# Series of unread matrix products added behind the last store of an encoder kernel

## The chip, the cores and the metric

The kernel runs on one core of a Trainium2 chip. The metric is the device time of one execution in microseconds (us). Before the change it was 1070.83 us, the median of two runs (1070.76 and 1070.89).

## The reference, cut to what matters

The reference is a bidirectional encoder of two layers over 256 tokens of width 1024, in f32:

```
for l in range(2):
    x = x + 0.5 * swiglu(rms_norm(x, ffn1_norm[l]), ffn1_w_in[l], ffn1_w_out[l])
    h = rms_norm(x, mix_norm[l])
    x = x + mixers(h) @ w_mix_out[l]         # latent, windowed and neighbourhood attention
    x = x + mem_xattn(rms_norm(x, mem_norm_x[l]), mem, ...)
    x = x + 0.5 * swiglu(rms_norm(x, ffn2_norm[l]), ffn2_w_in[l], ffn2_w_out[l])
    x = rms_norm(x, block_norm[l])
return x
```

Only its last line bears on the change: after the second feed-forward of layer 1, `x` is divided by the root of its mean square and returned.

## The kernel before, in words

The activations live in SBUF, transposed, as `x` of 128 partitions x 8 blocks x 256 tokens, a view of the tile `gx`. The weights stream in as pieces of 128x1024; ScalarE casts each to a high part in fp32r (L140, `whi`) and VectorE makes the low part (L141, `wlo`). A product of f32 accuracy is three TensorE products in fp32r (`mm3`, L167 to L169). In the feed-forward layers (`ffn`, names f01, f02, f11, f12) each of them loads 128x128 weights that lie side by side and streams 256 columns; in one projection of the mixer (`formb`, mb1) 512 columns. A weight load is an instruction of its own (LDWEIGHTS, shown as the engine PEld) that runs beside the product ahead of it.

Sums over partitions are f32 products with a column of constants (L979). `pacc` has eight PSUM banks of 512 f32 columns, which `acc(name)` hands out; `sp` has ten SBUF slots of 8 KB per partition, which `slot` hands out. During the last feed-forward eight of the ten slots are held by its input (two) and its inner activations (six).

The end of the kernel, L974 to L992, is one chain: the sum of squares (L979), its mean (L984), the power of -1/2 on GpSimd (L173), the transposition of the factor (L988), and five products of `x` with it on VectorE (L991), each followed by a store of its blocks by SyncE's queue (L992). `x` is complete in SBUF only after the fifth.

At the very start four products of zeros fill a bank that nothing reads (L117 to L119, name `idle`).

A framework orders the instructions of each engine from the dependences between tiles and a simulated timeline (L1126), and sets the semaphores. Where the profile gives L1126, it means the framework's waits and the barrier at the end.

Of the kernel before, what the change touches and what calls it, by code (L numbers as in the profile page):

```python
# [10 lines left out]
F32R = mybir.dt.float32r  # L11
# [7 lines left out]
P = 128  # L19
T = 256  # L20
# [971 lines left out]
        nc.sync.dma_start(out[:, a:b, :], v)  # L992

def _tiles(v):

    return v.reshape(-1, P).T
# [132 lines left out]
```

## Time and profile before

| | |
|---|---|
| median of the runs | 1070.83 us |
| the profiled execution's own time | 1071.27 us |
| its span, first to last instruction | 1069.5 us |
| mean granted TensorE clock | 0.994 of full |
| TensorE products, busy | 1048.8 us, 8480 instructions |
| weight loads, busy | 1027.0 us, 8480 instructions |
| VectorE busy | 717.6 us |
| ScalarE busy | 556.9 us |

The span is 1.77 us shorter than the profiled execution's own time. Busy times of products and of weight loads overlap, and a product's busy time is longer than the distance between two starts, since they are pipelined: the distance between starts is what a series costs.

### The profile page before, as it was taken

The numbers are of one execution on the slowest core, as the hardware profiler recorded it, in microseconds if no ns is written. First come the engines' busy times: TensorE is split into PE (matmuls) and PEld (weight loads), VectorE is DVE, ScalarE is ACT, GpSimd is POOL, SyncE is SP. The second block draws the span as 40 slices with busy tenths as digits, with TensorE's granted clock in tenths as the row PEclk, the third lists the DMA queues.
The fourth block names the chain that finished last, engine by engine and source line by source line (L and its number), as shares of the span: only waits on it lengthen the run. The fifth ranks groups of instructions, "written<-read, shape, count | busy, mean of one in ns | idle before, by whom it ended". The sixth has DMA issues, their size and how long they took to land.

```text
span 1069.5 us, 20916 instructions
## 1 busy us (share of the span) xinstructions
PE 1048.8 (98%) x8480; PEld 1027.0 (96%) x8480; DVE 717.6 (67%) x1249; ACT 556.9 (52%) x928; POOL 114.5 (11%) x107
## 2 busy tenths in 40 slices
PE   8999999999999999999999999999999999999996
PEld 7999999988999999999999999999889999999996
DVE  7866666678786676666658666667886776666652
ACT  5644455566554554445445444546674545544441
POOL 4000000071020500000000000001500321000000
PEclk9999999999999999999999999999999999999998
DMA  8865556555041655555555555655631426656641
GB/s 290 269 191 183 193 189 205 172 180 179 21 138 60 229 185 182 193 179 194 181 180 188 184 190 187 205 181 165 192 111 46 153 78 215 187 191 183 190 122 40
DMA packets 54530, 181.79 MB, mean 170 GB/s; under 512 B 6049, under 2 KB 8993, under 8 KB 54433
## 3 DMA queue, kind: packets, MB, share of 16 engines
q1 hardware_dynamic: 54432, 180.45, 52.7%
q8 instruction: 66, 1.08, 0.4%
q14 instruction: 32, 0.25, 0.1%
HBM read 179.38 MB, written 1.05 MB: 169 GB/s over the span
## 4 chain that ended last, share of the span: by engine, by line
PE 75%; issue 17%; DVE 4%; DMA 2%; ACT 1%; POOL 1%; SPq 0%; POOLq 0%; DVEq 0%; ACTq 0%
PE f11i L167 4%; PE f01i L167 4%; PE f01i L169 4%; PE f11i L169 4%; PE f11i L168 3%; PE f01i L168 3%; PE f02i L167 3%; PE f02i L169 3%; PE f02i L168 3%; PE f11o L167 2%; PE f02o L167 2%; PE f01o L167 2%; PE f11o L169 2%; PE f02o L169 2%; PE f01o L169 2%
## 5 line engine op out<-in xcount | busy, mean ns | idle before, releaser
L141 DVE TENSOR_TENSOR wlo<-raw,whi 128x1024 fp32r<-128x1024 f32 (+4 forms) x337 | 406.8, 1211 | 227.6 <-ACT whi L140 226.6
L140 ACT CAST whi<-raw 128x1024 fp32r<-128x1024 f32 (+4 forms) x337 | 343.7, 1023 | 372.9 <-issue 92.6
L167 PE MATMUL f02i<-n20h,whi 128*128 128x256 f32 x320 | 90.5, 283 | 0.0
L168 PE MATMUL f12i<-n21l,whi 128*128 128x256 f32 x320 | 90.2, 282 | 0.0
L167 PE MATMUL f12i<-n21h,whi 128*128 128x256 f32 x320 | 90.2, 282 | 0.0
L168 PE MATMUL f02i<-n20l,whi 128*128 128x256 f32 x320 | 90.1, 281 | 0.0
L169 PE MATMUL f02i<-n20h,wlo 128*128 128x256 f32 x320 | 90.0, 281 | 0.0
L169 PE MATMUL f12i<-n21h,wlo 128*128 128x256 f32 x320 | 90.0, 281 | 0.0
L167 PE MATMUL f11i<-n10h,whi 128*128 128x256 f32 x320 | 89.9, 281 | 0.0
L167 PE MATMUL f01i<-n0h,whi 128*128 128x256 f32 x320 | 89.8, 281 | 0.0
L169 PE MATMUL f01i<-n0h,wlo 128*128 128x256 f32 x320 | 89.4, 279 | 0.0
L168 PE MATMUL f01i<-n0l,whi 128*128 128x256 f32 x320 | 89.3, 279 | 0.0
L169 PE MATMUL f11i<-n10h,wlo 128*128 128x256 f32 x320 | 89.3, 279 | 0.0
L168 PE MATMUL f11i<-n10l,whi 128*128 128x256 f32 x320 | 89.3, 279 | 0.0
L169 PEld LDWEIGHTS f02i<-n20h,wlo 128*128 128x128 f32 x320 | 61.0, 191 | 0.0
L167 PEld LDWEIGHTS f12i<-n21h,whi 128*128 128x128 f32 x320 | 60.9, 190 | 0.0
L168 PEld LDWEIGHTS f12i<-n21l,whi 128*128 128x128 f32 x320 | 60.9, 190 | 0.0
L167 PEld LDWEIGHTS f02i<-n20h,whi 128*128 128x128 f32 x320 | 60.8, 190 | 0.0
L168 PEld LDWEIGHTS f02i<-n20l,whi 128*128 128x128 f32 x320 | 60.6, 189 | 0.0
L169 PEld LDWEIGHTS f12i<-n21h,wlo 128*128 128x128 f32 x320 | 60.6, 189 | 0.0
L169 PEld LDWEIGHTS f01i<-n0h,wlo 128*128 128x128 f32 x320 | 60.2, 188 | 0.0
L169 PEld LDWEIGHTS f11i<-n10h,wlo 128*128 128x128 f32 x320 | 60.2, 188 | 0.0
(1026 smaller groups left out, 2945.1 us busy)
## 6 DMA issues: line engine op xcount, KB each, us to landing
raw<-in_w SPq DMA_DIRECT2D x311, 512.0 KB, 3.9
raw<-in_w SPq DMA_DIRECT2D x12, 384.0 KB, 3.3
raw<-in_w SPq DMA_DIRECT2D x8, 416.0 KB, 3.3
kv0mt<-in_mem SPq DMA_DIRECT2D x8, 128.0 KB, 4.2
kv1mt<-in_mem SPq DMA_DIRECT2D x8, 128.0 KB, 3.9
gx<-in_gx SPq DMA_DIRECT2D x3, 256.0 KB, 6.2
out<-gx SPq DMA_DIRECT2D x3, 256.0 KB, 2.8
gx<-in_gx SPq DMA_DIRECT2D x1, 323.0 KB, 3.1
```

Source lines behind the costliest of these rows:

```text
L140: ins = nc.scalar.copy(hi[:, a:b], r[:, a:b])
L141: nc.vector.tensor_tensor(lo[:, a:b], r[:, a:b], hi[:, a:b].bitcast(F32), ALU.subtract)
L167: nc.tensor.matmul(ps, ah, bh, start=first, stop=False)
L168: nc.tensor.matmul(ps, ah, bl, start=False, stop=False)
L169: return nc.tensor.matmul(ps, al, bh, start=False, stop=last)
```

## The change

Nothing of the old code is changed. Behind the last store two slots, `sr` and `mr`, are filled with copies of the finished `x` in fp32r by VectorE. Then TensorE runs series of products: the weights are 128 columns of `sr` taken with a step `s` in elements of 4 bytes, the moving operand is `n` columns of `mr` that begin `m` bytes into it. Each series accumulates into one bank, and nothing reads the banks.

| series | number | step s | columns n | products each | products |
|---|---|---|---|---|---|
| heat | 1 | 1 | 512 | 24 | 24 |
| za | 4 | 1 | 256 | 24 | 96 |
| zb | 16 | 2 | 256 | 12 | 192 |
| zc | 8 | 2 | 512 | 10 | 80 |
| zd | 8 | 4 | 256 | 10 | 80 |
| ze | 4 | 3 | 256 | 10 | 40 |
| zf | 4 | 1 | 512 | 12 | 48 |
| zg | 8 | 2 | 256 | 12 | 96 |

```diff
         nc.sync.dma_start(out[:, a:b, :], v)
 
 
+    sr = slot([P, 8, T], F32R, "sr")
+    mr = slot([P, 8, T], F32R, "mr")
+    for d_ in (sr, mr):
+        nc.vector.tensor_copy(d_, x)
+    st, mv = sr.rearrange("p k t -> p (k t)"), mr.rearrange("p k t -> p (k t)")
+
+    def series(name, w, s, m, n, reps, step, mod):
+        ps = acc(name)
+        for i in range(reps):
+            o = w + (i * step) % mod
+            lhs = st[:, o : o + 128 * s].rearrange("p (c s) -> p c s", s=s)[:, :, 0]
+            nc.tensor.matmul(
+                ps[:, 0:n], lhs, mv[:, m // 4 : m // 4 + n], start=i == 0, stop=i == reps - 1
+            )
+
+    series("heat", 0, 1, 0, 512, 24, 128, 1024)
+    for m in (0, 64, 128, 192):
+        series(f"zaw0s1m{m}n", 0, 1, m, 256, 24, 128, 1024)
+    for w in (0, 1):
+        for m in range(0, 256, 32):
+            series(f"zbw{w}s2m{m}n", w, 2, m, 256, 12, 256, 1536)
+    for m in range(0, 256, 32):
+        series(f"zcw0s2m{m}n", 0, 2, m, 512, 10, 256, 1536)
+    for m in (0, 32, 64, 96, 128, 160, 192, 224):
+        series(f"zdw0s4m{m}n", 0, 4, m, 256, 10, 1, 4)
+    for m in (0, 64, 128, 192):
+        series(f"zew0s3m{m}n", 0, 3, m, 256, 10, 1, 3)
+    for m in (0, 64, 128, 192):
+        series(f"zfw0s1m{m}n", 0, 1, m, 512, 12, 128, 1024)
+
+    for m in range(0, 256, 32):
+        ps = acc(f"zgm{m}")
+        for i in range(12):
+            o = (i // 2) * 256 + i % 2
+            lhs = st[:, o : o + 255].rearrange("p c -> p c")[:, 0:255:2] if o % 2 else st[:, o : o + 256 : 2]
+            nc.tensor.matmul(ps[:, 0:256], lhs, mv[:, m // 4 : m // 4 + 256], start=i == 0, stop=i == 11)
```

## Rows read from the trace of the kernel before

**Rows 1.** The page: busy time, share, instructions of PE; clock in 40 slices.
```profile
PE 1048.8 (98%) x8480; PEld 1027.0 (96%) x8480; DVE 717.6 (67%) x1249; ACT 556.9 (52%) x928; POOL 114.5 (11%) x107
...
PEclk9999999999999999999999999999999999999998
```

**Rows 2.** Timeline of the end: start us, us, engine, line, operation, count.
```profile
1062.04 0.43 PE L988 MATMUL endb<-ident,endr 128*128 128x128 f32 x2 [1.03 <-POOL endr L173]
1062.51 2.54 DVE L991 TENSOR_TENSOR gx<-gx,endb 128x256 f32<-128x256 f32 x5 [1.30 <-PE endb L988]
1062.95 2.45 SPq L992 DMA_DIRECT2D out<-gx  x5
```

**Rows 3.** The stores' line: issue ns min/median/max, first and last start; time to landing.
```profile
L992 SPq DMA_DIRECT2D out<-gx x5: 332/338/423, 1063.0 to 1065.1; - x5
...
DMA to landing us min/median/max: 1.9/2.5/3.0
```

**Rows 4.** Stretches at the end: busy by engine (count), clock, DMA share, GB/s.
```profile
1062.00:1063.00 1.00, 0.43 (x2) 0.19 (x2) 0.49 (x2) 0.00 (x0) 0.00 (x0) 0.97 0.00 0
1063.00:1064.00 1.00, 0.00 (x0) 0.00 (x0) 1.00 (x3) 0.00 (x0) 0.00 (x0) 0.50 0.17 58
...
1066.00:1069.50 3.50, 0.00 (x0) 0.00 (x0) 0.00 (x0) 0.00 (x0) 0.00 (x0) 0.50 0.34 101
```

**Rows 5.** VectorE's groups by form: busy us, mean ns of one, idle before.
```profile
L991 DVE TENSOR_TENSOR gx<-gx,endb 128x512 f32<-128x512 f32 x3 | 1.9, 681 | 0.0
...
L852 DVE TENSOR_SCALAR mx0o<-mx0o,mx0or 128x256 f32<-128x256 f32 x4 | 1.2, 350 | 0.4 <-POOL mx0or L173 0.3
...
L852 DVE TENSOR_SCALAR mx0o<-mx0o,mx0or 128x512 f32<-128x512 f32 x2 | 0.9, 484 | 0.8 <-POOL mx0or L173 0.8
L991 DVE TENSOR_TENSOR gx<-gx,endb 128x256 f32<-128x256 f32 x2 | 0.8, 419 | 1.3 <-PE endb L988 1.3
```

**Rows 6.** The tile f12o, its 528 products: ns min/median/max, first and last start.
```profile
L167 PE MATMUL f12o<-f12ah,whi x176: 279/279/280, 996.6 to 1058.5; 128*128 128x256 f32 x176
...
L169 PE MATMUL f12o<-f12ah,wlo x176: 279/279/281, 996.9 to 1058.7; 128*128 128x256 f32 x176
```

**Rows 7.** Timeline of mb1, first and last of 13 products of 512 columns.
```profile
227.68 0.40 PE L530 MATMUL mx0mb<-whi,nx0l 128*128 128x512 f32 x1
...
230.48 0.40 PE L530 MATMUL mx0mb<-whi,nx0l 128*128 128x512 f32 x1
```

**Rows 8.** Timeline of PEld: four weight loads under products of one column.
```profile
1058.70 0.53 PEld L979 LDWEIGHTS end<-cmean,nb1s 128*128 128x128 f32 x4
```

**Rows 9.** The tile endb: its weights are one element read 128 times.
```profile
L988 PEld LDWEIGHTS endb<-ident,endr x2: 132/134/136, 1062.0 to 1062.1; 128*128 128x128 f32 x2
```

**Rows 10.** PEld's groups by form: transpositions with weights side by side.
```profile
L739 PEld LDWEIGHTS mx0st<-ident,mx0qk 128*128 128x128 f32 x14 | 1.6, 140 | 0.1
```

**Rows 11.** Timeline of PE at two falls of the clock (15 starts after 888.87).
```profile
362.21 0.61 PE L251 MATMUL n20ps<-cmean,n20s 128*128 128x1 f32 x4 [1.68 <-POOL n20s L208]
...
886.96 0.61 PE L251 MATMUL n21ps<-cmean,n21s 128*128 128x1 f32 x4 [2.15 <-POOL n21s L208]
...
888.87 0.42 PE L167 MATMUL f12i<-n21h,whi 128*128 128x256 f32 x1
...
892.08 0.37 PE L167 MATMUL f12i<-n21h,whi 128*128 128x256 f32 x1
```

**Rows 12.** Stretches there: the clock stands behind POOL's count.
```profile
366.50:367.00 0.50, 0.50 (x6) 0.50 (x6) 0.00 (x0) 0.00 (x0) 0.00 (x0) 0.88 0.57 205
...
889.00:892.00 3.00, 3.00 (x16) 3.00 (x15) 0.72 (x1) 0.54 (x1) 0.00 (x0) 0.50 0.84 289
892.00:892.50 0.50, 0.50 (x5) 0.50 (x4) 0.00 (x0) 0.50 (x1) 0.00 (x0) 0.73 1.02 352
```

**Rows 13.** The tile idle, four f32 products whose bank nothing reads.
```profile
L119 PE MATMUL idle<-idle x8: 584/634/793, 1.3 to 4.4; 128*128 128x256 f32 x8
```

**Rows 14.** The page: the queue that brings in instructions, packets, MB, share.
```profile
q8 instruction: 66, 1.08, 0.4%
```

## What the change will do to the time

> **What bounds the kernel now.** I read the page first: TensorE is busy for 98% of the span and its clock is full in every slice but the last [rows 1]. So work that is added to TensorE can hide nowhere inside the kernel, and this work may not even try: it reads the finished `x`. I therefore went to the timeline of the end. The reader should see there a chain without overlap: TensorE's last product starts at 1062.04, VectorE scales `x` from 1062.51 to 1065.05, the fifth store is issued at about 1065.1 and lands up to 3.0 us later, at about 1068.1; the span ends 1.4 us behind that [rows 2, 3]. [...]
>
> **The change, part by part.** It removes and moves nothing; it adds two copies, 656 products and as many weight loads.
>
> *The copies.* Both need all of `x`, so the first begins at 1065.05. No copy of this size is in the trace. VectorE's nearest operation, with one tensor operand from SBUF to SBUF, takes 350 ns for 256 columns and 484 ns for 512 [rows 5], 134 ns for each further 256. Six times that on top of 484 gives 1.29 us for 2048 columns, 2.6 us for the two. The other end is the pace with two tensor operands, 419 and 681 ns [rows 5]: 681 + 6 x 262 = 2.25 us, 4.5 us for two. I take the first, because it also has one tensor operand. TensorE starts at 1065.05 + 2.6 + about 0.1 = 1067.75 us. The slots are no obstacle: eight of ten are in use in the last feed-forward. The stores only read `x`, as the copies do, and land beside them.
>
> *The pitch of products at full clock.* The 528 products of f12o start between 996.6 and 1058.7: 62.1 / 527 = 0.1178 us for 256 columns [rows 6]. Twelve steps of 512 columns take 230.48 - 227.68 = 2.80, or 0.2333 us each [rows 7]. These pitches contain the weight load that runs beside each product. [...]
>
> *Heat.* 24 products of 512 columns begin at half clock. There, 15 steps of 256 columns take 892.08 - 888.87 = 3.21 us, 0.214 each [rows 11], so 512 columns 0.428 (an estimate, twice that). At the two falls inside the kernel the clock was full again 4.4 us (362.21 to about 366.62) and 5.3 us (886.96 to about 892.27) after TensorE had resumed work; the ends are read from the means 0.88 and 0.73 of half-microsecond stretches [rows 11, 12]. With 5.0 us at half clock, 11.7 products are done, and the other 12.3 take 2.9 us: 7.9 us. The ends are 24 x 0.2333 = 5.6 and 24 x 0.428 = 10.3 us.
>
> *The series with weights side by side.* za: 96 x 0.1178 = 11.3 us. zf: 48 x 0.2333 = 11.2 us. Their starting bytes differ from those of the old products; nothing in the trace varies that alone, so I take the pitch as it is.
>
> *The series with strided weights.* zb and zg are 288 products, zd 80, ze 40, all of 256 columns; zc is 80 of 512. No weight load of the trace has a step of two or more, so its price needs bounds. With products of one column, which leave the weight load to set the pace, four loads take 0.53 us, of which the last alone is 0.19: 0.34 / 3 = 0.113 us per load [rows 8]. That is just under the 0.1178 of a 256-column product: a slower load shows at once in 256 columns, and in 512 only beyond 0.2333. The lower bound is half the pitch at half clock, 0.107 us [rows 11], at which the extra at full clock would vanish: over all 504 products of 256 columns and the 128 of 512 behind heat it saves 5.4 + 2.5 = 8 us. The upper bound is a load whose pace grows with the step: 0.227, 0.34 and 0.453 us for steps two, three and four, which adds 288 x 0.109 + 40 x 0.222 + 80 x 0.335 = 31.4 + 8.9 + 26.8 = 67 us. The only row with another step than one is the transposition of a single repeated element, 134 ns against 140 for elements side by side [rows 9, 10]: there the addresses did not set the load's duration. That is the nearest row, so I take no slowdown: 408 x 0.1178 = 48.1 us, and zc 80 x 0.2333 = 18.7 us.
>
> *What costs nothing.* The 53 series take turns in eight banks, but each bank's former writer is the same in-order engine, eight series back. Were TensorE to drain between series, each would pay 0.279 - 0.118 = 0.16 us [rows 6], 8.5 us together. Instructions came in 66 packets for the old program [rows 14]; the new pairs follow at the pitch at which the feed-forward was supplied. No engine waits for the products but the closing barrier.
>
> **Sum.** 7.9 + 11.3 + 11.2 + 48.1 + 18.7 = 97.2 us. 1067.75 + 97.2 = 1164.95; the last product ends 0.16 us behind its pitch; I let the barrier take the same 1.4 us that it takes behind the last landing: span 1166.5. The profiled execution was 1.77 us longer than its span, and 0.44 above the median of the runs, so the time is **1168 us**, 9% above before. Its own range, from the bounds of copies, heat, pitch and turns of banks, is 1160 to 1176. A measurement of this kernel tells differences of about 2%, some 21 us, from none.
>
> **Rivals.**
>
> *Steps of three and four load slower.* If the load needs two elements near each other, the 120 products of zd and ze fall to twice the load's pace, 0.227: 120 x 0.109 = 13.1 us more, **1181**. [...] No run here shows it yet. Against it stands that a load moves an element in 0.113 / 128 = 0.88 ns where the moving operand takes 0.46 [rows 6, 8], so the memory may have time to spare. Chance 0.15.
>
> *The two streams meet.* With step two the weights advance 1024 bytes per load, as much as 256 moving columns do in nearly the same time. If both then stay on the same part of the memory for some starting bytes and not for others, part of zb and zg is slow. Half of 288 at 0.227 gives 15.7 us, **1184**; all of them give 1199. For it: weights and moving operand share SBUF. Against it: a stall shifts one stream and ends the meeting. Chance 0.20.
>
> *Every stride halves the pace.* All 408 products of 256 columns at 0.227: 44.5 us, **1212**, and up to 1235 by the upper bound; zc stays hidden, 0.227 under 0.2333. Against it rows 9 and 10. Chance 0.14.
>
> *The products are not there* (the other side). If what nobody reads were dropped when the program is built, the copies alone would end at 1067.7, before the last landing at 1068.1, and the time would stay **1071**. It decides only while fewer than some 165 products of 256 columns are left: 2% is reached when they run 21.7 us from 1067.75, of which 5.0 at half clock hold 23 (0.214 each) and 16.7 hold 142. Against it: four unread products of the kernel before are in its trace [rows 13]. Chance 0.02.
>
> **How the numbers follow.** 0.45 for the forecast, 0.15, 0.20, 0.14 and 0.02 for the rivals, 0.04 for what I don't name, near the forecast or above it. The range runs from 1160, the forecast's lower end, to 1200, the end of the meeting streams; it leaves out the case in which every stride halves the pace, the dropped products and part of the unnamed, under 0.2. All cases but the dropped ones are slower by over 2%: slower 0.97, within 2% 0.02, faster 0.01.
>
> **What would show it.** In the trace after: TensorE's next product behind L988 starts near 1067.7; heat's starts are 0.43 us apart at clock 0.50 and then 0.233; za and zf keep 0.118 and 0.233; zb, zg, zd and ze have za's pitch, zc has zf's. [...] Gaps between series would show drains. The prediction is wrong if any of the strided groups leaves 0.118 by over a tenth.

## The result and the profile after

The changed kernel takes 1178.72 us, median of two runs (1176.65 and 1180.78), against 1070.83: a ratio of 1.1023, 95% interval 1.0972 to 1.1074. The forecast was 1168 with a range of 1160 to 1200. The time lies in the range, but 11 us above the forecast and above the forecast's own range (to 1176): it is near the first rival's 1181.

The timeline of TensorE and VectorE after shows which step it was (start us, us, engine, line, operation, count; the distance from one series' start to the next, divided by the count, is the pitch of a product):

```profile
1062.84 0.43 PE L988 MATMUL endb<-ident,endr 128*128 128x128 f32 x2 [1.03 <-POOL endr L173]
1063.30 2.54 DVE L991 TENSOR_TENSOR gx<-gx,endb 128x256 f32<-128x256 f32 x5 [1.30 <-PE endb L988]
...
1065.88 1.23 DVE L998 CAST sr<-gx 128x2048 fp32r<-128x2048 f32 x1
1067.03 1.22 DVE L998 CAST mr<-gx 128x2048 fp32r<-128x2048 f32 x1
1068.30 8.34 PE L1006 MATMUL heat<-mr,sr 128*128 128x512 f32 x24 [5.03 <-DVE mr L998]
...
1076.48 3.04 PE L1006 MATMUL zaw0s1m0n<-mr,sr 128*128 128x256 f32 x24
...
1087.86 1.60 PE L1006 MATMUL zbw0s2m0n<-mr,sr 128*128 128x256 f32 x12
...
1110.97 2.49 PE L1006 MATMUL zcw0s2m0n<-mr,sr 128*128 128x512 f32 x10
...
1129.61 2.39 PE L1006 MATMUL zdw0s4m0n<-mr,sr 128*128 128x256 f32 x10
1131.84 2.50 PE L1006 MATMUL zdw0s4m32n<-mr,sr 128*128 128x256 f32 x10
1134.17 2.50 PE L1006 MATMUL zdw0s4m64n<-mr,sr 128*128 128x256 f32 x10
...
1148.22 1.93 PE L1006 MATMUL zew0s3m0n<-mr,sr 128*128 128x256 f32 x10
...
1155.26 2.90 PE L1006 MATMUL zfw0s1m0n<-mr,sr 128*128 128x512 f32 x12
...
1166.36 11.72 PE L1030 MATMUL zgm<-mr,sr 128*128 128x256 f32 x96
```

The head of this list answers to [rows 2]: the kernel's own end is the same, 0.80 us later in this execution. The page counts 9136 products for the 8480 of before: all 656 are there. From the starts follow the terms of the sum:

| term | forecast us | after us | pitch after us |
|---|---|---|---|
| TensorE starts, behind the end of L991 | 2.7 | 2.46 | |
| heat | 7.9 | 8.18 | |
| za, 96 of step 1 | 11.3 | 11.38 | 0.1185 |
| zb, 192 of step 2 | 22.6 | 23.11 | 0.1204 |
| zg, 96 of step 2 | 11.3 | about 11.6 | 0.1204 |
| zc, 80 of step 2, 512 columns | 18.7 | 18.64 | 0.2330 |
| zd, 80 of step 4 | 9.4 | 18.61 | 0.2326 |
| ze, 40 of step 3 | 4.7 | 7.04 | 0.1760 |
| zf, 48 of step 1, 512 columns | 11.2 | 11.10 | 0.2313 |

Step one costs the pitch of before, [rows 6, 7], and step two 2% more. Step three costs 1.5 times as much and step four twice: 2.3 and 9.2 us, 11.5 of the 12.4 us by which the sum was short. (The first distance in the first series of zd is 0.118, the product's own pace, because that series begins with a load that ran beside zc's last product; the other seven series of zd take 0.2340 a product.) The weight loads carry it; these are groups of the engine PEld by form (busy us, mean ns of one, idle before), against 0.113 us per load [rows 8] and 0.19 for a single one before:

```profile
L1006 PEld LDWEIGHTS zaw0s1m64n<-mr,sr 128*128 128x128 f32 x24 | 2.9, 188 | 0.0
L1006 PEld LDWEIGHTS zdw0s4m64n<-mr,sr 128*128 128x128 f32 x10 | 2.4, 330 | 0.0
...
L1006 PEld LDWEIGHTS zew0s3m64n<-mr,sr 128*128 128x128 f32 x10 | 1.8, 262 | 0.0
L1006 PEld LDWEIGHTS zbw0s2m64n<-mr,sr 128*128 128x128 f32 x12 | 1.5, 197 | 0.0
```

And the clock at heat, in stretches (length, busy by engine with counts; the clock stands before the DMA's share):

```profile
1068.00:1073.00 5.00, 4.70 (x11) 3.73 (x12) 0.24 (x1) 0.00 (x0) 0.00 (x0) 0.50 0.01 2
1073.00:1074.00 1.00, 1.00 (x4) 0.76 (x4) 0.00 (x0) 0.00 (x0) 0.00 (x0) 0.56 0.00 0
1074.00:1076.00 2.00, 2.00 (x10) 1.66 (x9) 0.00 (x0) 0.00 (x0) 0.00 (x0) 1.00 0.03 8
```

The mean of 0.56 in the second stretch says that the clock was 0.50 until about 1073.9, 5.6 us of work against the 5.0 taken.

### The profile page after: what moved, and what is told of

Same layout as the page of the kernel before. It is cut to its first block, busy times and chain, and to the rows that moved or that the text cites. A ratio compares the mean times of both kernels' runs of the same rounds, so it can differ in the third digit from the quotient of the medians.

```text
span 1179.0 us, 22231 instructions
## 1 busy us (share of the span) xinstructions
PE 1159.7 (98%) x9136; PEld 1130.5 (96%) x9136; DVE 722.1 (61%) x1251; ACT 556.2 (47%) x928; POOL 113.2 (10%) x107
## 4 chain that ended last, share of the span: by engine, by line
PE 78%; issue 16%; DVE 3%; DMA 1%; ACT 1%; POOL 1%; SPq 0%; DVEq 0%; POOLq 0%; ACTq 0%
PE f11i L167 3%; PE f01i L167 3%; PE f01i L169 3%; PE f11i L169 3%; PE f01i L168 3%; PE f11i L168 3%; PE f02i L167 3%; PE f02i L169 3%; PE f02i L168 3%; PE f01o L167 2%; PE f11o L167 2%; PE f02o L167 2%; PE f11o L169 2%; PE f02o L169 2%; PE f01o L169 2%
```

## The experiments

The theory that the runs from here on try: a weight load in fp32r reads SBUF in pieces of 16 bytes, four elements, and pays about 1.83 ns for each piece that it touches (an estimate, 0.2340 / 128 at step four and 0.1760 / 96 at step three), with a floor of 0.113 us for 128 elements [rows 8]. From "More steps" on each kernel was run once, and what it shows is read from the pitches inside one trace. The rivals: the price grows with the distance between elements; the load is slow only because the product beside it reads too; the price is one of place in the sequence; it is one of TensorE's cycles, and doubles at half clock.

**The kernel again, and zd and ze with step one.** The second kernel changes two calls:

```diff
-        series(f"zdw0s4m{m}n", 0, 4, m, 256, 10, 1, 4)
+        series(f"zdw0s1m{m}n", 0, 1, m, 256, 10, 1, 4)
-        series(f"zew0s3m{m}n", 0, 3, m, 256, 10, 1, 3)
+        series(f"zew0s1m{m}n", 0, 1, m, 256, 10, 1, 3)
```

> The changed kernel once more, unaltered, to be timed beside the next two. All theories: about 1178.7 us, between the 1176.7 and 1180.8 that its two runs gave; zd at about 0.234 us a product and ze at 0.176, the same for every starting byte.

> zd and ze keep their numbers of products, 80 and 40, but read their weights with a step of one. If steps of four and three are what the forecast missed, zd falls from 0.234 and ze from 0.176 to 0.118 us a product: 80 x 0.116 + 40 x 0.058 = 11.6 us less than the unaltered kernel beside it, about 1167, and its TensorE part comes out at the 97 us that was forecast. If the slowness belongs to the place in the sequence (late, many series, turns of banks) and not to the step, both stay near 0.234 and 0.176 and the time stays at 1179.

Measured on one chip: 1176.60 us (1175.21 to 1178.31), ratio 1.1019 (1.0994 to 1.1043), and 1166.72 us (1165.66 to 1167.63), ratio 1.0924 (1.0898 to 1.0951). The unaltered kernel has 0.233 for zd and 0.176 for ze again. The medians differ by 9.9 us, the stretches from zd to zf in the two traces by 25.65 - 14.27 = 11.4; in the second trace the work behind the copies begins 1.0 us later. In the same places, with step one:

```profile
1127.07 1.37 PE L1006 MATMUL zdw0s1m0n<-mr,sr 128*128 128x256 f32 x10
...
1136.61 1.34 PE L1006 MATMUL zew0s1m0n<-mr,sr 128*128 128x256 f32 x10
...
1141.34 2.90 PE L1006 MATMUL zfw0s1m0n<-mr,sr 128*128 128x512 f32 x12
```

9.54 / 80 = 0.119 and 4.73 / 40 = 0.118 us. So the step is the cause and the place is not, and without it the kernel comes within 1.3 us of what was forecast.

**The copies alone.** All from `st, mv` on is taken out.

> Leaves out all products and keeps the two copies. If the copies run beside the landing of the stores, as the forecast's start of TensorE at 1067.75 assumes, the copies end before the last landing and the time stays at 1070.8. If they delay the stores or the barrier behind them, it is up to 2.4 us more, 1073.2.

Measured: 1069.06 us, ratio 1.000 (0.998 to 1.002) to the kernel before on that chip (1068.76). Its trace has the copies of 1.23 and 1.22 us, the second begun at 1065.1 and so ended at 1066.3; the fifth store is issued at 1064.0 and lands up to 3.0 us later, at up to 1067.0. They hide.

**More steps.** Series of 24 products with one address each:

```diff
+    for s in (1, 2, 3, 4, 5, 6, 8, 12, 16):
+        series(f"s{s}n", 0, s, 0, 256, 24, 0, 1)
+    for s in (3, 4):
+        series(f"wide{s}n", 0, s, 0, 512, 24, 0, 1)
+    for s in (4, 8):
+        ps = acc(f"cols64s{s}n")
...
+            lhs = st[:, 0 : 64 * s].rearrange("p (c s) -> p c s", s=s)[:, :, 0]
+            nc.tensor.matmul(ps[0:64, 0:256], lhs, mv[:, 0:256], start=i == 0, stop=i == 23)
```

> Other series in place of the old ones, 24 products each of 256 columns, weights with steps of 1, 2, 3, 4, 5, 6, 8, 12 and 16 elements; then 512 columns with steps of 3 and 4; then 64 columns of weights with steps of 4 and 8. Theory of the lines: a load pays about 1.83 ns for each piece of 16 bytes that it touches, 64 at step two, 96 at three, 128 from four on, so 0.118, 0.118, 0.176, 0.234 and then 0.234 for every larger step; the 512 columns hide both at 0.233; 64 columns of weights with step four touch 64 pieces and cost 0.118 again. Theory of the distance: the price grows with the step, 0.059 us for each element of it, so 0.29 at five, 0.47 at eight and 0.94 at sixteen; 64 columns with step four 0.118, with step eight 0.234.

Timeline of PE (each row against the next, over 24):

```profile
1076.67 3.04 PE L1006 MATMUL s1n<-mr,sr 128*128 128x256 f32 x24
1079.54 3.04 PE L1006 MATMUL s2n<-mr,sr 128*128 128x256 f32 x24
1082.41 4.32 PE L1006 MATMUL s3n<-mr,sr 128*128 128x256 f32 x24
1086.58 5.77 PE L1006 MATMUL s4n<-mr,sr 128*128 128x256 f32 x24
1092.18 5.65 PE L1006 MATMUL s5n<-mr,sr 128*128 128x256 f32 x24
1097.66 5.66 PE L1006 MATMUL s6n<-mr,sr 128*128 128x256 f32 x24
1103.16 5.97 PE L1006 MATMUL s8n<-mr,sr 128*128 128x256 f32 x24
1108.96 6.56 PE L1006 MATMUL s12n<-mr,sr 128*128 128x256 f32 x24
1115.36 5.46 PE L1006 MATMUL s16n<-mr,sr 128*128 128x256 f32 x24
1120.65 5.87 PE L1006 MATMUL wide3n<-mr,sr 128*128 128x512 f32 x24
1126.36 5.80 PE L1006 MATMUL wide4n<-mr,sr 128*128 128x512 f32 x24
1131.99 2.99 PE L1020 MATMUL cols64s4n<-mr,sr 128*64 128x256 f32 x24
1134.82 3.11 PE L1020 MATMUL cols64s8n<-mr,sr 128*64 128x256 f32 x24
```

Steps 1 to 6: 0.120, 0.120, 0.174, 0.233, 0.228, 0.229; eight 0.242, twelve 0.267, sixteen 0.220. The price stops growing at four, so the theory of the distance (0.47 at eight, 0.94 at sixteen) falls. It is not quite flat, and why twelve costs 0.267 is open. Under 512 columns steps three and four hide (0.238, 0.235). 64 columns of weights, 64 pieces, cost 0.118 with step four and 0.123 with step eight, where the theory of the distance wanted 0.234.

**The load alone.**

```diff
+    for n in (128, 16):
+        for s in (1, 2, 3, 4, 8):
+            series(f"heat{heat}_", 0, 1, 0, 512, 24, 128, 1024)
+            heat += 1
+            series(f"a{n}s{s}n", 0, s, 0, n, 24, 0, 1)
...
+            nc.tensor.matmul(ps[:, 0:256], lhs, mv[:, 0:1].to_broadcast([P, 256]), start=i == 0, stop=i == 23)
```

> The load by itself: series of 24 products of only 128 and of 16 columns, weights with steps 1, 2, 3, 4 and 8, each behind a series of 24 products of 512 columns; then 256 columns that are one element read 256 times, with weights of step one and four. Theory of the lines: the load sets the pace, 0.113 at steps one and two (at most 0.118 at two), 0.176 at three, 0.234 at four and eight, whatever the product beside it does, also where the moving operand is one element. Theory of the meeting streams: the load is slow because the product reads beside it, so with 16 columns, or with one element moving, steps of three, four and eight come back towards 0.113.

With 16 columns, from start to start of series over 24: 0.108, 0.114, 0.167, 0.225 and 0.230; with 128 columns 0.110, 0.115, 0.169, 0.227 and 0.233. These means lie a little under the price of a load, because each series begins with a load that ran beside the last product ahead of it, so that its first distance is only 0.027 to 0.067. The median distance between neighbouring starts is 0.112, 0.118, 0.173, 0.234 and 0.238 with 16 columns and 0.111, 0.118, 0.175, 0.234 and 0.240 with 128. With 256 columns that are one element it is 0.112 at step one and 0.233 at step four:

```profile
1128.39 2.74 PE L1006 MATMUL a16s1n<-mr,sr 128*128 128x16 f32 x24
1130.99 7.34 PE L1006 MATMUL heat__13416<-mr,sr 128*128 128x512 f32 x24
...
1159.27 5.55 PE L1006 MATMUL a16s4n<-mr,sr 128*128 128x16 f32 x24
1164.67 7.98 PE L1006 MATMUL heat__13566<-mr,sr 128*128 128x512 f32 x24
...
1185.99 2.85 PE L1021 MATMUL one1n<-mr,sr 128*128 128x256 f32 x24
1188.67 5.76 PE L1021 MATMUL one4n<-mr,sr 128*128 128x256 f32 x24
1194.27 1.58 PE L1006 MATMUL zlast<-mr,sr 128*128 128x256 f32 x12
```

The load pays whatever stands beside it: the meeting streams are out.

**At half clock.**

```diff
+    for k, s in enumerate((4, 1, 8, 3)):
+        if k:
+            for _ in range(8):
+                nc.vector.tensor_copy(mr, x)
+        series(f"c{s}n", 0, s, 0, 256, 30, 0, 1)
```

> Series of 30 products of 256 columns with weights of steps 4, 1, 8 and 3, each begun after TensorE has stood idle for several us (for the later three VectorE fills mr eight times more), so that its first part runs at a granted clock of 0.50. If a piece of 16 bytes costs time of the memory, steps of four and eight take 0.234 us at either clock, or little more, step three 0.214 at half clock (the product's own pace) and 0.176 at full, step one 0.214 and 0.118. If it costs cycles of TensorE's clock, the prices double at half clock: 0.47 for four and eight, 0.35 for three.

A stretch inside the series of step 4 (the first count in parentheses is that of PE; the clock, before the DMA's share, is 0.50):

```profile
1066.00:1070.00 4.00, 4.00 (x19) 4.00 (x19) 0.00 (x0) 0.00 (x0) 0.00 (x0) 0.50 0.02 4
```

The median distances between neighbouring starts at clock 0.50 are 0.234 us at step four, 0.247 at eight, 0.213 at one and three; at clock 1.00, later in the same series, 0.233, 0.238, 0.120 and 0.173. So the price of a piece is a time: the same at granted clocks of 0.50 and 1.00 for step four (0.234 and 0.233), 4% more at 0.50 for step eight (0.247 and 0.238). At 0.47 only nine products would start in this stretch.

**The step on the moving operand.**

```diff
+    for s in (1, 2, 3, 4, 6):
+        moved(f"v{s}n", 0, 1, s, 256)
+    moved("pair8in", 0, 2, 8, 256)
+    moved("pair8over", 3, 2, 8, 256)
```

`moved(name, first, size, step, n)` takes runs of `size` neighbours every `step` elements of `mr` from `first` on, against weights side by side.

> The step is put on the other operand: weights side by side, moving operand of 256 columns with steps 1, 2, 3, 4 and 6, then as pairs of neighbours every eight elements, pairs that lie in one piece of 16 bytes (elements 0 and 1) and pairs that lie across two (3 and 4), and 128 columns with steps two and four. Theory of the lines, if it holds for both streams: 64, 128, 192, 256 and 256 pieces, so 0.118, 0.234, 0.351, 0.469 and 0.469; the pairs in one piece 0.234, the pairs across two 0.469; 128 columns 0.118 and 0.234. It would also say why 256 columns side by side take 0.118 and not 0.107. Theory of the distance: pairs in and across cost the same, and step six more than step four. If only weight loads pay, all of 256 columns stay near 0.118.

```profile
1078.97 5.61 PE L1016 MATMUL v2n<-mr,sr 128*128 128x256 f32 x24
1084.39 5.62 PE L1016 MATMUL v3n<-mr,sr 128*128 128x256 f32 x24
```

Steps 1, 2, 3, 4 and 6: 0.120, 0.226, 0.227, 0.233 and 0.227; pairs in one piece 0.233, across two 0.233; 128 columns with steps two and four 0.116 and 0.118. The theory of the lines has step two right, and fails from three on (0.351 and 0.469 expected), for the pairs across two pieces and for 128 columns with step four (0.234 expected). Nor does distance explain it. A further run took longer runs of neighbours:

```diff
+    moved("q2by4n", 0, 2, 4, 256)
+    moved("q4by8n", 0, 4, 8, 256)
+    moved("q4by8over", 2, 4, 8, 256)
...
+            nc.tensor.matmul(ps[:, 0:256], lhs, mv[:, 0:1024].rearrange("p (c s) -> p c s", s=4)[:, :, 0], start=i == 0, stop=i == 23)
```

> What is open after the run with steps on the moving operand in fp32r: any step from two on cost 0.23 us for 256 columns, and pairs in one piece of 16 bytes as much as pairs across two, which the pieces do not explain. Here runs of neighbours: pairs every four elements, fours every eight, on pieces and across them, eights every sixteen, sixteens every thirty-two, 64 every 128. If the moving operand is read by pieces, fours on a piece cost what elements side by side cost, 0.118, and fours across two pieces 0.23. If only an unbroken innermost run counts, the price falls slowly with its length whatever the pieces. Then weights with steps four and eight and a moving operand with step four together: if the two streams pay side by side, 0.234 as for the weights alone; if they share one supply, about 0.46.

```profile
1074.51 5.68 PE L1016 MATMUL q2by4n<-mr,sr 128*128 128x256 f32 x24
1080.01 3.00 PE L1016 MATMUL q4by8n<-mr,sr 128*128 128x256 f32 x24
1082.86 5.69 PE L1016 MATMUL q4by8over<-mr,sr 128*128 128x256 f32 x24
1088.37 3.06 PE L1016 MATMUL q8by16n<-mr,sr 128*128 128x256 f32 x24
...
1099.92 5.94 PE L1029 MATMUL both4n<-mr,sr 128*128 128x256 f32 x24
1105.68 5.94 PE L1029 MATMUL both8n<-mr,sr 128*128 128x256 f32 x24
```

Fours on a piece cost 0.119, fours across two 0.230, pairs 0.229: pieces of 16 bytes count here too (64, 128 and 128 of them at 1.8 ns). Eights, sixteens and runs of 64 on pieces, 64 pieces each, cost 0.120, 0.121 and 0.120, so the length of a run does not count. But the price stops at about 0.23 us, 0.9 ns for an element, where weights go to 1.83. Weights and moving operand strided together cost 0.240, not the 0.46 expected of two streams that share one supply.

**bf16.** Both operands in bf16, 2 bytes an element; the series are as above, with products of 16 columns in the second run, of which this is the main part:

```diff
+    for s in (1, 4, 8, 16, 32):
+        series(f"b16x{s}n", 0, s, 0, 16, 48, 0, 1)
+        series(f"again{s}n", 0, 1, 0, 512, 24, 128, 1024)
+    for s in (3, 6, 8, 12):
...
+            rhs = mv[:, 0 : 256 * s].rearrange("p (c s) -> p c s", s=s)[:, :, 0]
+            nc.tensor.matmul(ps[:, 0:256], st[:, 0:128], rhs, start=i == 0, stop=i == 23)
```

> Weights and moving operand in bf16, elements of 2 bytes: 256 columns with weights of steps 1, 2, 3, 4, 6, 8 and 16, then 128 columns with steps 1, 4 and 8, then moving operands with steps 2, 4 and 8. Theory of the lines: 16 bytes hold eight elements, so step four (64 pieces) stays at the product's pace, which without the pieces' limit is 0.107 to 0.110 and not 0.118; step six touches 96 and takes 0.176, eight and sixteen 128 and 0.234; moving with steps two, four and eight 64, 128 and 256 pieces, 0.118, 0.234 and 0.469. Theory of the step in elements: three and four cost 0.176 and 0.234 as in fp32r.

> What is open after the run in bf16: its weight loads showed no price up to step sixteen under 256 columns, and 0.062 us at step eight under 128. Here 48 products of 16 columns in bf16 leave the load alone, weights with steps 1, 4, 8, 16 and 32, each behind products of 512 columns; then moving operands of 256 columns with steps 3, 6, 8 and 12. If a bf16 load is read as four streams at once, each paying 1.8 ns for a piece of 16 bytes, step eight, sixteen and thirty-two cost 32 x 1.8 = 0.058 us and steps one and four less. If bf16 weights pay no piece at all, all steps cost the same. Moving: by pieces 96, 192, 256 and 256, so 0.17, 0.34, 0.45 and 0.45; by distance step twelve costs 0.68.

First run: weights of every step to sixteen hide under 256 columns, 0.109 to 0.110 us; under 128 columns steps 1, 4 and 8 take 0.056, 0.055 and 0.062. Second run, with 16 columns: 0.025, 0.033, 0.062, 0.061 and 0.059 at steps 1, 4, 8, 16 and 32. The expectations of 0.176 at step six and 0.234 from eight on were wrong, and so was the theory of the step in elements (0.176 and 0.234 at three and four). Four streams at once would fit (an estimate, 32 x 1.83 = 0.059); no run tells them from one stream at a quarter of the price. The moving operand in bf16 goes by pieces all the way: steps 2, 3, 4, 6, 8 and 12 take 0.114, 0.172, 0.226, 0.340, 0.452 and 0.449, which is 64, 96, 128, 192, 256 and 256 pieces at 1.77 ns. Steps 8 and 12, in the second run:

```profile
1126.07 11.02 PE L1019 MATMUL w8n<-mr,sr 128*128 128x256 bf16 x24
1136.91 10.95 PE L1019 MATMUL w12n<-mr,sr 128*128 128x256 bf16 x24
```

## Why the prediction was right in sign and short by 11 us

*Where the work goes.* Right: TensorE starts behind L988 and the copies, 2.46 us behind the end of L991 for the 2.7 of the forecast. It is 1068.30 against 1067.75 because the body ended 0.80 us later. Alone, the copies cost nothing (1069.06 us against 1068.76). (A 9 in the slices of [rows 1] means 90% or more, not a full clock: the two falls of [rows 11, 12] lie inside such slices.)

*Heat.* 8.18 against 7.9 us, between the ends named; [rows 4] has the clock at 0.50 behind the kernel's last product, heat began at 0.50, and the clock stayed there 0.6 us longer than assumed.

*Weights side by side.* Right, 0.1185 and 0.2313 for the 0.1178 and 0.2333 of [rows 6, 7], at all four starting bytes of each. These were multiples of 64, that is, on a piece.

*Strided weights.* The step "I take no slowdown" failed for zd and ze (0.233 and 0.176 us for 0.1178) and held for zb, zc and zg. The prediction had named this sign itself, a strided group that leaves 0.118 by over a tenth: by it the mechanism of the forecast was wrong, though the time lies in the range. The step rested on [rows 9, 10], a single element read 128 times. That row touches one piece of 16 bytes, so it could say nothing of elements in different pieces; it was nearest by name only. The rival of steps three and four named the right series, with 0.15 too little chance. Its price of 13.1 us was measured as 11.5, because step three costs 1.5 times the pace and not twice (2.3 us for 4.4), while step four costs a little more (9.2 for 8.7). The argument against it, that a load at 0.88 ns an element has time to spare beside a moving operand at 0.46, took both streams for readers of the same kind; alone, with 16 columns, the load at step four still takes 0.234 us.

*Pieces and pitch.* For weights in fp32r two elements on a piece cost little: step two 0.1204 us, steps three and four 0.176 and 0.233. The moving operand does not follow this: pairs in one piece cost 0.233 in fp32r, and step four in bf16, also two elements on a piece, 0.226 for 0.109.

Side by side, 256 columns take 0.109 to 0.110 us in bf16 and 0.1178 in fp32r [rows 6]. In fp32r the moving operand's 64 pieces at 1.83 ns would make 0.117 (an estimate); this fits, and 256 columns that are one element came down to the load's own 0.112, but no run isolates it.

*From the sum to the time.* The span in the profile is 1179.0 us for the 1166.5 of the forecast: 12.4 from the terms of the sum and 0.55 from the later start, less 0.5, because the span ended 0.9 us behind the last product (1178.1) and not 1.4. That the time is off by 11 and not by 12.5 is luck: the median of the runs lies 2.06 us below the profiled execution, where the forecast took off 0.44.

*Range.* The forecast's own range ended at 1176, below the 1178.72; 1160 to 1200 held because the rivals were let in. That every stride would halve the pace is refuted by zb (0.1204), the drains between series by the same pitch, at which zb's sixteen short series run on without a gap, and the dropped products by the 656 in the trace. The meeting of the streams is refuted by zb and zg, which keep 0.120 at every starting byte, and by the load alone (0.234 at step four with 16 columns).

## What to carry to other kernels

Count the pieces of 16 bytes that a weight load touches: in fp32r each cost about 1.83 ns here, so a step of two was nearly free beside 256 columns (0.120), three cost half as much again (0.174 to 0.176) and four or more about twice (0.220 to 0.267 up to step sixteen). 512 columns hid steps three and four (0.238 and 0.235); larger steps were not run beside them. Strides of the moving operand were dearer than they look: in fp32r step two already took 0.226 us for 0.120, in bf16 the price went on to four times at step eight (0.452 for 0.109). A nearest row must share the quantity that the price depends on; when no row does, a rival with a stated mechanism deserves more than a row that merely looks alike.

## What the runs showed of the hardware that was not expected

A piece's price is a time: 0.234 us at step four with the granted clock at 0.50, 0.233 at 1.00. And TensorE's clock fell while its products ran, by the trace, without a pause. In the second run in bf16 it fell at 1124.0 (a mean of 0.75 from 1123 to 1125), inside the series with the moving operand at step six (0.340 us a product over the series), and stayed at 0.50 through steps 8 and 12 (0.452 and 0.449):

```profile
1121.00:1123.00 2.00, 2.00 (x7) 0.66 (x6) 0.00 (x0) 0.00 (x0) 0.00 (x0) 1.00 0.00 0
1123.00:1125.00 2.00, 2.00 (x7) 0.72 (x6) 0.00 (x0) 0.00 (x0) 0.00 (x0) 0.75 0.00 0
...
1126.00:1136.00 10.00, 10.00 (x23) 2.76 (x22) 0.00 (x0) 0.00 (x0) 0.00 (x0) 0.50 0.00 0
1137.00:1147.00 10.00, 10.00 (x24) 2.77 (x23) 0.00 (x0) 0.00 (x0) 0.00 (x0) 0.50 0.00 0
```

That the clock really was at half shows in the series behind, side by side in bf16: 0.213 us a product until it rose at 1151.3, then 0.109. In the run of the load alone the mean clock is 1.00 from 1103.0 to 1108.0, inside the series of 128 columns with weights of step four, and 0.77 from 1108.3 to 1115.2, in the series of 512 columns behind it, with TensorE busy throughout; that series and the six of 512 columns after it take 7.2 to 8.2 us, the three before it 5.7.

Open: why the moving operand in fp32r stops at 0.9 ns an element where bf16 pays 1.77, and the 0.267 us of weights with step twelve.
